# HGRN scores and outputs written between the k tiles of the projections that follow

## The chip, the cores and the metric

The kernel runs on one core of a Trainium2 chip. A core has five engines with a queue each: PE (TensorE, matrix products; the profile shows its weight loads apart, as PEld), DVE (VectorE, elementwise), ACT (ScalarE, functions and scaled copies), POOL (GpSimd) and SP (SyncE, which here issues the DMAs of the weights). PE writes to PSUM, from which DVE and ACT read. An engine runs its queue in order; an instruction that waits holds up those behind it on the same engine. The metric is the device time in microseconds; lower is better.

## The reference, cut to what matters

The input has 256 tokens of width 2048. It is normalised and multiplied by one wide weight matrix, whose columns are split into projections. Of these matter here `hq`, `hf` (query and forget gate of the HGRN branch), `hi`, `hg` (its value and output gate), and `aq`, `ak`, `av` of the attention branch. The HGRN branch has 8 heads of 128:

```python
f = sigmoid(hf); g = lb + (1 - lb) * f; log_g = log(g); kk = 1 - g
q = silu(hq) * HG_DK ** -0.5
# for each chunk of 64 tokens, S carried from chunk to chunk:
b = cumsum(log_g)
o_inter = (q * exp(b)) @ S
scores[t, s] = sum_k q[t, k] * exp(b[t, k] - b[s, k]) * kk[s, k]      # s <= t
o = o_inter + scores @ v
S = exp(b_last) * S + (kk * exp(b_last - b)).T @ v
# then
y_a = rms_norm(o, hg_norm_w) * silu(hg)
```

The attention branch, the gated merge of both branches, an output projection and a squared-ReLU MLP follow; the change does not touch them.

## The kernel before, in words

All large products are computed in three parts: each weight tile is read as f32 (`raw`), ACT casts it to a short form (`wh`, line 89), DVE takes the difference (`wl`, line 90), and PE adds up hi x hi, hi x lo and lo x hi. `weights` (line 109) makes these tiles, 16 k tiles to a projection, and asks SP for their DMAs. `gemm` (line 150) is a projection of 512 columns with tokens as rows (`hi`, `hg`, `av`); each k tile takes six matmuls of 128x512. `gemm_t` (line 158) is one of 256 columns with the transposed result (`hf`, `hq`, `aq`, `ak`); each k tile takes four matmuls (lines 170 to 174). Their accumulators are two buffers of two PSUM banks.

The eight HGRN heads are worked in four pairs `u` = 0 to 3, two pairs to a group of 512 columns. `fq(u)` runs the projections `hf` and `hq` of a pair (those of pairs 0 and 1 run earlier) and makes the gate, `kk`, the scan `b` and the query `q`. `v_chunk(g)` and `hg_chunk(g)` run `hi` and `hg` of a group. `hgrn_scores` (line 346) makes the decayed scores of a pair, without a loop over chunks, in five parts:

- blocks of one token: `kk` x `q` into PSUM (line 353), read by DVE into `sd` (lines 354, 355);
- three levels with blocks of 2, 8 and 32 tokens. For each, DVE and ACT make factors `kl` and `qr` (lines 363 to 386), PE multiplies them (line 393, four f32 products, each two instructions of 128x192), and DVE copies what a mask selects into `sd` (line 400, three copies a head);
- the lower left block of 128 x 128 tokens: factors `kc`, `ql` (lines 405 to 416), PE (line 419), and a copy by ACT into `so` (line 422).

`hgrn_out` (line 427) computes a pair's output: PE multiplies the scores by `v` into `po` (lines 439, 440), ACT squares (line 443), DVE and POOL make the reciprocal root (lines 95, 96), DVE scales and gates into `o` (line 450). It returns `finish`, which transposes `o` on PE into `tpo` (line 458) and splits it into the activations `ya` (lines 460, 461). Score tiles and `po` tiles share two PSUM buffers of one bank each (the tag `sm`); a pair's `po` needs both.

Two things set the order. The first is the order in which the program writes its instructions, at the end of the stage (lines 481 to 498). The second is the planner of the framework: in its own model of time it gives every engine, at each point, the instruction that was written first among those whose inputs and buffers are ready by then. The order so made is fixed in each engine's queue. Blocks under `high_priority` count as if written 2000 instructions earlier; the splitting of weights and the emptying of some accumulators are such blocks. So instructions of the scores that are written early may run before, and PE may fit pieces of a later projection between them.

Of the kernel before, what the change touches and what calls it, by code (L numbers as in the profile page):

```python
# [8 lines left out]
F32 = mybir.dt.float32  # L9
# [41 lines left out]
def tile_hybrid_block(  # L51
# [95 lines left out]
    def lhs_of(lhs, kt, m):  # L147
        return [lhs[kt // 4][:, kt % 4, u, m * P:(m + 1) * P] for u in range(2)]

    def gemm(lhs, w, n0, nkt, what, wide=False):  # L150

        acc = new_acc(what)
        for kt, wh, wl in weights(w, n0, nkt, NC, what, wide=wide):
            for m in range(NM):
                mm3(acc[:, m, :], *lhs_of(lhs, kt, m), wh, wl, kt == 0, kt == nkt - 1)
        return acc

    def gemm_t(rhs, w, n0, nkt, what):

        acc = new_acc(what)  # L160
        for a in weights(w, n0, nkt, T, what):
            mm_t(acc, rhs, nkt, *a)
        return acc

    def mm_t(acc, rhs, nkt, kt, wh, wl):
        r = rhs[kt // 4][:, kt % 4]
        for cb in range(2):
            c = slice(cb * P, (cb + 1) * P)
            if kt:
                nc.tensor.matmul(acc[:, cb, 0:T], wl[:, c], r[:, 0, :], start=False, stop=False)  # L170
            nc.tensor.matmul(acc[:, cb, :], wh[:, c], r.rearrange("p u t -> p (u t)"),  # L171
                             start=kt == 0, stop=kt == nkt - 1)
            if kt == 0:
                nc.tensor.matmul(acc[:, cb, 0:T], wl[:, c], r[:, 0, :], start=False, stop=False)
# [149 lines left out]
            nc.vector.tensor_tensor(q[:, h, :, P:], odd(q[:, :, :, 0:P])[:, h], odd(half(g))[:, h], op=ALU.mult)  # L324
        return q

    def v_chunk(g):
        acc = gemm(xT, w_in_n, C_HI + g * NC, KD, f"hi{g}")
        vs = []
        for m in range(NM):  # L330
            v = hp.tile([P, NC], F32, name=f"v{g}{m}", tag="tok", bufs=7)
            nc.scalar.activation(v, acc[:, m, :], AF.Copy, scale=rstd[:, m:m + 1])
            vs.append(v)
        return vs

    def hg_chunk(g):
        acc = gemm(xT, w_in_n, C_HG + g * NC, KD, f"hg{g}")
        gws = []
        for m in range(NM):
            s = hp.tile([P, NC], F32, name=f"gw{g}{m}", tag="tok", bufs=7)  # L340
            nc.scalar.activation(s, acc[:, m, :], AF.Sigmoid, scale=rstd[:, m:m + 1])
            nc.vector.scalar_tensor_tensor(s, acc[:, m, :], rstd[:, m:m + 1], s, op0=ALU.mult, op1=ALU.mult)
            gws.append(s)
        return gws

    def hgrn_scores(n, kk, b, q):

        sd = hp.tile([P, 2, NM, P], F32, name=f"sd{n}", tag="sd", bufs=2)

        for h in range(2):  # L350
            ps = ps_sm.tile([P, NM, 192], F32, name=f"ps{n}_1{h}", tag="sm")
            for m in range(NM):
                nc.tensor.matmul(ps[:, m, :], kk[:, h, m * P:(m + 1) * P], q[:, h, m, :], start=True, stop=True)
            nc.vector.tensor_tensor(sd[:, h], ps[:, :, 0:P], bc(ident, 1, NM), op=ALU.mult)
            nc.vector.copy_predicated(sd[:, h].rearrange("p m (j u) -> p m j u", u=2)[:, :, :, 1],
                                      bc(mask1.bitcast(I32), 1, NM), ps[:, :, P:])

        for i, B in enumerate(LEVELS):
            npar = 2 * T // (4 * B)
            blocks = lambda a: a.rearrange("p h t -> p (h t)").rearrange("p (n v b) -> p n v b", v=4, b=B)  # L360
            bv = blocks(b)
            end = bv[:, :, :, B - 1]
            el = hp.tile([P, npar, 4, B], F32, name=f"el{n}_{B}", tag="e", bufs=2)
            nc.vector.tensor_tensor(el, bc(end, 3, B), bv, op=ALU.subtract)
            nc.scalar.activation(el, el, AF.Exp)
            kl = hp.tile([P, npar, 4, B], F32, name=f"kl{n}_{B}", tag="kl", bufs=3)
            nc.vector.tensor_tensor(kl, blocks(kk), el, op=ALU.mult)
            er = hp.tile([P, npar, 4, B], F32, name=f"er{n}_{B}", tag="e", bufs=2)
            rr = hp.tile([P, npar, 4], F32, name=f"rr{n}_{B}", tag=f"rr{B}", bufs=2)
            if B < CH // 2:  # L370
                nc.vector.tensor_tensor(er[:, :, 1:4, :], bv[:, :, 1:4, :], bc(end[:, :, 0:3], 3, B), op=ALU.subtract)
                nc.scalar.activation(er[:, :, 1:4, :], er[:, :, 1:4, :], AF.Exp)
                nc.vector.tensor_tensor(rr[:, :, 1:3], end[:, :, 1:3], end[:, :, 0:2], op=ALU.subtract)
                nc.scalar.activation(rr[:, :, 1:3], rr[:, :, 1:3], AF.Exp)
            else:
                two = lambda a, j: a.rearrange("p n (w j) b -> p n w j b", j=2)[:, :, :, j, :]
                nc.vector.tensor_tensor(two(er, 1), two(bv, 1), bc(two(bv, 0)[:, :, :, B - 1], 3, B), op=ALU.subtract)
                nc.scalar.activation(two(er, 1), two(er, 1), AF.Exp)
                nc.scalar.activation(two(er, 0), two(bv, 0), AF.Exp)
                nc.vector.tensor_copy(rr, er[:, :, :, B - 1])  # L380
            qr = hp.tile([P, npar, 6, B], F32, name=f"qr{n}_{B}", tag="qr", bufs=2)
            wide = lambda a, k: a.rearrange("p (a n) k b -> p a n (k b)", n=32 // B)[:, :, :, k]
            qv = q[:, :, :, 0:P].rearrange("p h m t -> p (h m) t").rearrange("p a (n w) -> p a n w", w=4 * B)
            nc.vector.tensor_tensor(wide(qr, slice(0, 3 * B)), qv[:, :, :, B:], wide(er, slice(B, 4 * B)), op=ALU.mult)
            nc.vector.tensor_tensor(qr[:, :, 3:5, :], qr[:, :, 1:3, :], bc(rr[:, :, 1:3], 3, B), op=ALU.mult)
            nc.vector.tensor_tensor(qr[:, :, 5, :], qr[:, :, 4, :], bc(rr[:, :, 1], 2, B), op=ALU.mult)
            klf = kl.rearrange("p n v b -> p (n v b)")
            qrf = qr.rearrange("p n k b -> p (n k b)")
            for h in range(2):
                ps = ps_sm.tile([P, NM, 192], F32, name=f"ps{n}_{B}{h}", tag="sm")  # L390
                for m in range(NM):
                    a = 2 * h + m
                    nc.tensor.matmul(ps[:, m, :], klf[:, a * P:(a + 1) * P], qrf[:, a * 192:(a + 1) * 192],  # L393
                                     start=True, stop=True)
                dst = sd[:, h].rearrange("p m (n w) -> p m n w", w=4 * B)
                src = ps.rearrange("p m (n w) -> p m n w", w=6 * B)
                mask = masks[:, i, :].rearrange("p (n w) -> p n w", w=6 * B).bitcast(I32)
                for d0, k0, k1 in ((1, 0, 3), (2, 3, 5), (3, 5, 6)):
                    k = slice(k0 * B, k1 * B)
                    nc.vector.copy_predicated(dst[:, :, :, d0 * B:], bc(mask[:, :, k], 1, NM), src[:, :, :, k])  # L400

        heads = lambda a: a.rearrange("p (h m) v b -> p h m v b", m=NM)
        r = rr.rearrange("p (h m) v -> p h m v", m=NM)
# [10 lines left out]
        ql = hp.tile([P, 2, 4, 32], F32, name=f"ql{n}", tag="ql", bufs=1)  # L414
        nc.vector.tensor_tensor(ql[:, :, 0, :], q[:, :, 1, 0:32], heads(er)[:, :, 1, 0, :], op=ALU.mult)
        nc.vector.tensor_tensor(ql[:, :, 1:4, :], heads(qr)[:, :, 1, 0:3, :], bc(d128[:, :, 1:4], 3, 32), op=ALU.mult)
        ps = ps_sm.tile([P, 2, P], F32, name=f"ps{n}_128", tag="sm")
        for h in range(2):
            nc.tensor.matmul(ps[:, h, :], kc[:, h].rearrange("p v b -> p (v b)"),
                             ql[:, h].rearrange("p v b -> p (v b)"), start=True, stop=True)  # L420
        so = hp.tile([P, 2, P], F32, name=f"so{n}", tag="so", bufs=2)
        nc.scalar.copy(so, ps)
        return sd, so

    ya = []

# [35 lines left out]

        return finish

    def fq(u):
        if u == 0:
            f, z = f0, z0
        elif u == 1:
            f, z = f1, z1
        else:  # L470
            f, z = h2(f"f{u}"), h2(f"zq{u}")
            add_parts(f, gemm_t(xT, w_in_t, C_HF + u * T, KD, f"hf{u}"))
            add_parts(z, gemm_t(xT, w_in_t, C_HQ + u * T, KD, f"hq{u}"))
        g, kk, b = hf_pair(u, f)
        return kk, b, hq_pair(u, z, g)


    def hgrn_group(g, s0, s1, vs, gws):
        return hgrn_out(g, 0, s0, vs, gws), hgrn_out(g, 2, s1, vs, gws)

    ya += [new_act(f"ya{g}") for g in range(2)]
    a0, a1 = fq(0), fq(1)
    vs0 = v_chunk(0)
    gws0 = hg_chunk(0)
    s0 = hgrn_scores(0, *a0)
    a2 = fq(2)
    s1 = hgrn_scores(1, *a1)
    a3 = fq(3)
    o0 = hgrn_group(0, s0, s1, vs0, gws0)
    vs1 = v_chunk(1)  # L490
    for finish in o0:
        finish()
    s2 = hgrn_scores(2, *a2)
    gws1 = hg_chunk(1)
    s3 = hgrn_scores(3, *a3)
    acc_q0 = gemm_t(xT, w_in_t, C_AQ, KD, "aq00")
    for finish in hgrn_group(1, s2, s3, vs1, gws1):
        finish()
    hpool_cm.__exit__(None, None, None)


# [527 lines left out]
```

## Time and profile before

| | |
|---|---|
| median of 3 runs | 1424.85 us (1422.13 to 1425.19) |
| the profiled execution | 1427.49 us |
| its span, first to last instruction | 1425.8 us |
| mean granted clock of TensorE | 0.997 |
| PE busy | 1404.3 us |
| DVE busy | 1147.7 us |
| ACT busy | 855.0 us |
| first score matmul to last, in the span | 98.37 to 227.9 us |
| `po` matmuls | 155.7 to 236.9 us |
| transposes of the outputs | 184.6 to 242.4 us |

Busy time is the sum of an engine's instructions, overlaps counted once; matmuls overlap, and their ends are modelled. In a row of the timeline stand the start, the length, the engine, the line, the operation and its tiles, and in brackets how long the engine had been idle before and which instruction released it. In a row of the groups `x96` is a count and the last column the idle time before them. In the windows each row is a stretch; the granted clock is 1.00 where PE runs at full speed.

### The profile page before, as it was taken

The page shows a single profiled execution, that of the slowest core. Times are in us where ns is not written, and L with a number is a line of the kernel's source. Part 1 is how long each engine was busy: PE and PEld are TensorE (multiplying, and loading weights), DVE is VectorE, ACT ScalarE, POOL GpSimd, SP SyncE. Part 2 cuts the span into 40 slices and gives each one's busy share as a digit, 9 for nine tenths or more (in the row PEclk, how much of TensorE's full clock was granted, in tenths as well). Part 3 has the DMA queues.
Part 4 walks back from the last instruction along what each step waited for, and adds up shares of the span by engine and source line. Part 5 has one row for each costly group of instructions (what it writes and reads, how often), then busy time and mean ns, then how long its engine had stood idle before and what let it go on. Part 6 is the DMA issues. An engine that isn't in the chain of part 4 may idle for free.

```text
span 1425.8 us, 18422 instructions
## 1 busy us (share of the span) xinstructions
PE 1404.3 (98%) x6629; PEld 1162.4 (82%) x6629; DVE 1147.7 (80%) x1506; ACT 855.0 (60%) x1132; POOL 33.9 (2%) x92
## 2 busy tenths in 40 slices
PE   9999999999999999999999999999999999999997
PEld 7888788878787888888888878888788888888886
DVE  7779886675758885688998978979788998889984
ACT  6766744464556664446666765566556775557753
POOL 2000001010000000000000000000000000000000
PEclk9999999999999999999999999999999999999999
DMA  9654444565556657656654566555576555667542
GB/s 315 231 192 148 134 161 133 189 177 167 163 177 222 212 185 226 202 194 222 207 191 133 192 223 215 182 187 177 184 236 236 178 167 173 234 223 237 180 146 103
DMA packets 122156, 272.83 MB, mean 191 GB/s; under 512 B 10192, under 2 KB 31440, under 8 KB 121680
## 3 DMA queue, kind: packets, MB, share of 16 engines
q1 hardware_dynamic: 119328, 264.80, 56.0%
q0 software_dynamic: 1584, 5.25, 1.4%
q10 hardware_dynamic: 1152, 1.60, 0.3%
q8 instruction: 52, 0.85, 0.2%
q14 instruction: 40, 0.33, 0.1%
HBM read 269.51 MB, written 2.10 MB: 190 GB/s over the span
## 4 chain that ended last, share of the span: by engine, by line
PE 77%; DVE 10%; DMA 5%; ACT 3%; issue 3%; SPq 1%; POOL 0%; POOLq 0%; ACTq 0%; DVEq 0%
PE acc_ak L171 2%; PE acc_aq L171 2%; DVE raw_dn L702 2%; PE acc_hf L171 1%; PE acc_hq L171 1%; PE ps L393 1%; PE acc_hg L145 1%; PE acc_hg L144 1%; PE acc_hg L143 1%; PE acc_ba L145 1%; PE acc_bb L143 1%; PE acc_av L145 1%; PE acc_bb L144 1%; PE acc_ba L144 1%; PE acc_av L143 1%
## 5 line engine op out<-in xcount | busy, mean ns | idle before, releaser
L171 PE MATMUL acc_hf<-act_x,wh_hf 128*128 128x512 f32 x128 | 47.2, 405 | 1.3 <-DVE f L179 1.3
L171 PE MATMUL acc_aq<-act_x,wh_aq 128*128 128x512 f32 x128 | 47.1, 404 | 0.0
L171 PE MATMUL acc_hq<-act_x,wh_hq 128*128 128x512 f32 x128 | 45.9, 398 | 0.0
L171 PE MATMUL acc_ak<-act_x,wh_ak 128*128 128x512 f32 x128 | 45.0, 397 | 0.0
L702 DVE TENSOR_TENSOR raw_up<-raw_up,raw_up 128x1024 f32<-128x1024 f32 x32 | 39.1, 1221 | 0.5
L702 DVE TENSOR_TENSOR raw_dn<-raw_dn,raw_dn 128x1024 f32<-128x1024 f32 x32 | 39.0, 1218 | 0.2
L90 DVE TENSOR_TENSOR wl_ga<-raw_ga,wh_ga 128x1024 fp32r<-128x1024 f32 x16 | 19.6, 1225 | 19.6 <-ACT wh_ga L89 19.6
L170 PE MATMUL acc_aq<-act_x,wl_aq 128*128 128x256 f32 x120 | 35.1, 293 | 0.0
L170 PE MATMUL acc_hf<-act_x,wl_hf 128*128 128x256 f32 x120 | 34.8, 290 | 0.0
L90 DVE TENSOR_TENSOR wl_av<-raw_av,wh_av 128x1024 fp32r<-128x1024 f32 x16 | 19.6, 1224 | 18.1 <-ACT wh_av L89 18.1
L170 PE MATMUL acc_ak<-act_x,wl_ak 128*128 128x256 f32 x120 | 33.6, 280 | 0.0
L170 PE MATMUL acc_hq<-act_x,wl_hq 128*128 128x256 f32 x120 | 33.6, 280 | 0.0
L90 DVE TENSOR_TENSOR wl_ba<-raw_ba,wh_ba 128x1024 fp32r<-128x1024 f32 x16 | 19.6, 1224 | 16.6 <-ACT wh_ba L89 16.6
L89 ACT CAST wh_ba<-raw_ba 128x1024 fp32r<-128x1024 f32 x16 | 16.9, 1053 | 24.3 <-PE acc_ba L145 10.0
L90 DVE TENSOR_TENSOR wl_bb<-raw_bb,wh_bb 128x1024 fp32r<-128x1024 f32 x16 | 19.6, 1222 | 14.7 <-ACT wh_bb L89 14.7
L89 ACT CAST wh_bb<-raw_bb 128x1024 fp32r<-128x1024 f32 x16 | 16.9, 1054 | 22.8 <-PE acc_ba L145 12.7
L89 ACT CAST wh_av<-raw_av 128x1024 fp32r<-128x1024 f32 x16 | 16.8, 1052 | 22.0 <-PE acc_av L145 12.4
L90 DVE TENSOR_TENSOR wl_aq<-raw_aq,wh_aq 128x1024 fp32r<-128x1024 f32 x16 | 19.6, 1224 | 12.6 <-ACT wh_aq L89 12.6
L171 PEld LDWEIGHTS acc_hf<-act_x,wh_hf 128*128 128x128 f32 x128 | 24.2, 189 | 6.5 <-DVE f L179 1.6
L171 PEld LDWEIGHTS acc_hq<-act_x,wh_hq 128*128 128x128 f32 x128 | 24.0, 188 | 5.5
L171 PEld LDWEIGHTS acc_ak<-act_x,wh_ak 128*128 128x128 f32 x128 | 23.9, 188 | 5.5
L171 PEld LDWEIGHTS acc_aq<-act_x,wh_aq 128*128 128x128 f32 x128 | 24.1, 188 | 5.2 <-issue 0.7
(1626 smaller groups left out, 5107.3 us busy)
## 6 DMA issues: line engine op xcount, KB each, us to landing
raw_up<-in_w_up_dram SPq DMA_DIRECT2D x32, 512.0 KB, 5.4
raw_dn<-in_w_down_dram SPq DMA_DIRECT2D x32, 512.0 KB, 5.6
raw_ga<-in_w_in_t_dram SPq DMA_DIRECT2D x20, 512.0 KB, 4.4
raw_hi<-in_w_in_n_dram SPq DMA_DIRECT2D x16, 512.0 KB, 4.5
raw_hg<-in_w_in_n_dram SPq DMA_DIRECT2D x16, 512.0 KB, 3.7
raw_aq<-in_w_in_t_dram SPq DMA_DIRECT2D x16, 512.0 KB, 4.3
raw_ak<-in_w_in_t_dram SPq DMA_DIRECT2D x16, 512.0 KB, 3.6
raw_av<-in_w_in_n_dram SPq DMA_DIRECT2D x16, 512.0 KB, 4.3
```

The source lines that it names most:

```text
L89: (copy or nc.scalar.copy)(hi, src)
L90: nc.vector.tensor_tensor(lo, src, hi.bitcast(F32), op=ALU.subtract)
L143: nc.tensor.matmul(acc, hi, wh, start=first, stop=False, skip_group_check=True)
L144: nc.tensor.matmul(acc, hi, wl, start=False, stop=False, skip_group_check=True)
L145: nc.tensor.matmul(acc, lo, wh, start=False, stop=last, skip_group_check=True)
L170: nc.tensor.matmul(acc[:, cb, 0:T], wl[:, c], r[:, 0, :], start=False, stop=False)
L171: nc.tensor.matmul(acc[:, cb, :], wh[:, c], r.rearrange("p u t -> p (u t)"), start=kt == 0, stop=kt == nkt - 1)
L393: nc.tensor.matmul(ps[:, m, :], klf[:, a * P:(a + 1) * P], qrf[:, a * 192:(a + 1) * 192], start=True, stop=True)
L702: nc.vector.tensor_tensor(dst, dst, t, op=ALU.add)
```

## The change

No instruction of the computation is added or removed. `hgrn_scores` becomes a generator that stops at six places, and `gemm` and `gemm_t` take a list `between` of pairs (k tile, function): before the matmuls of that k tile are written, the function is called once. The first stop is after the factors of the level of 2; then come the blocks of one token and the factors of 8; the matmuls of level 2 and the factors of 32; those of level 8 and the factors `kc`, `ql`; those of level 32; and the block of 128. Factors are thus written one step ahead of the matmuls that use them, where before each level's factors stood right ahead of its matmuls.

Where each is written, with its k tiles:

| | before | after |
|---|---|---|
| scores of pair 0 | behind `hg0` | inside `hg0`, at 0, 5, 7, 9, 11, 13 |
| scores of pair 1 | behind `hq2` and the work of pair 2 | inside `hf2` at 0, 2, 6, 11 and `hq2` at 1, 6 |
| output of pair 0 | behind `hq3` and the work of pair 3 | inside `hq2` at 12 |
| output of pair 1 | right behind that of pair 0 | inside `hf3` at 8 |
| transposes of pairs 0 and 1 | behind `hi1` | inside `hq3` at 6 and 12 |
| scores of pair 2 | behind `hi1` and those transposes | inside `hi1` at 0, 5, 7, 9, 11, 13 |
| scores of pair 3 | behind `hg1` | inside `hg1` at 0, 5, 7, 9, 11, 13 |
| output of pair 2 | behind `aq00` | inside `aq00` at 6 |
| output of pair 3, both transposes | behind `aq00` | behind `aq00` |

```diff
-    def gemm(lhs, w, n0, nkt, what, wide=False):
+    def gemm(lhs, w, n0, nkt, what, wide=False, between=None):
 
         acc = new_acc(what)
         for kt, wh, wl in weights(w, n0, nkt, NC, what, wide=wide):
+            if between and between[0][0] == kt:
+                between.pop(0)[1]()
             for m in range(NM):
                 mm3(acc[:, m, :], *lhs_of(lhs, kt, m), wh, wl, kt == 0, kt == nkt - 1)
         return acc
 
-    def gemm_t(rhs, w, n0, nkt, what):
+    def gemm_t(rhs, w, n0, nkt, what, between=None):
 
         acc = new_acc(what)
         for a in weights(w, n0, nkt, T, what):
+            if between and between[0][0] == a[0]:
+                between.pop(0)[1]()
             mm_t(acc, rhs, nkt, *a)
         return acc
...
-    def hgrn_scores(n, kk, b, q):
+    def hgrn_scores(n, kk, b, q, out):
 
         sd = hp.tile([P, 2, NM, P], F32, name=f"sd{n}", tag="sd", bufs=2)
 
-        for h in range(2):
...
-        for i, B in enumerate(LEVELS):
+        def factors(B):
+
             npar = 2 * T // (4 * B)
...
+            return kl, qr, er, rr
+
+        def level(i, B, kl, qr):
             klf = kl.rearrange("p n v b -> p (n v b)")
...
+        made = factors(LEVELS[0])
+        yield
+
+        for h in range(2):
+            ps = ps_sm.tile([P, NM, 192], F32, name=f"ps{n}_1{h}", tag="sm")
+            for m in range(NM):
+                nc.tensor.matmul(ps[:, m, :], kk[:, h, m * P:(m + 1) * P], q[:, h, m, :], start=True, stop=True)
...
+        for i, B in enumerate(LEVELS):
+            kl, qr, er, rr = made
+            if i < len(LEVELS) - 1:
+                made = factors(LEVELS[i + 1])
+                yield
+                level(i, B, kl, qr)
...
+        yield
+        level(len(LEVELS) - 1, B, kl, qr)
+        yield
         ps = ps_sm.tile([P, 2, P], F32, name=f"ps{n}_128", tag="sm")
...
-        return sd, so
+        out += [sd, so]
+        yield
...
-    def hgrn_group(g, s0, s1, vs, gws):
-        return hgrn_out(g, 0, s0, vs, gws), hgrn_out(g, 2, s1, vs, gws)
-
     ya += [new_act(f"ya{g}") for g in range(2)]
-    a0, a1 = fq(0), fq(1)
-    vs0 = v_chunk(0)
-    gws0 = hg_chunk(0)
-    s0 = hgrn_scores(0, *a0)
-    a2 = fq(2)
-    s1 = hgrn_scores(1, *a1)
-    a3 = fq(3)
-    o0 = hgrn_group(0, s0, s1, vs0, gws0)
-    vs1 = v_chunk(1)
-    for finish in o0:
-        finish()
-    s2 = hgrn_scores(2, *a2)
-    gws1 = hg_chunk(1)
-    s3 = hgrn_scores(3, *a3)
-    acc_q0 = gemm_t(xT, w_in_t, C_AQ, KD, "aq00")
-    for finish in hgrn_group(1, s2, s3, vs1, gws1):
-        finish()
+    a, sc, vs, gws, ends = [None] * 4, [[] for _ in range(4)], [None] * 2, [None] * 2, []
+
+    def scores(u, *at):
+
+        steps = hgrn_scores(u, *a[u], sc[u])
+        return [(k, lambda: next(steps)) for k in at]
+
+    def outputs(u):
+        ends.append(hgrn_out(u // 2, u % 2 * 2, sc[u], vs[u // 2], gws[u // 2]))
+
+    def end():
+        ends.pop(0)()
+
+    a[0], a[1] = fq(0), fq(1)
+    vs[0] = v_chunk(0)
+    gws[0] = hg_chunk(0, scores(0, 0, 5, 7, 9, 11, 13))
+    s1 = scores(1, 0, 2, 6, 11, 1, 6)
+    a[2] = fq(2, s1[:4], s1[4:] + [(12, lambda: outputs(0))])
+    a[3] = fq(3, [(8, lambda: outputs(1))], [(6, end), (12, end)])
+    vs[1] = v_chunk(1, scores(2, 0, 5, 7, 9, 11, 13))
+    gws[1] = hg_chunk(1, scores(3, 0, 5, 7, 9, 11, 13))
+    acc_q0 = gemm_t(xT, w_in_t, C_AQ, KD, "aq00", [(6, lambda: outputs(2))])
+    outputs(3)
+    end()
+    end()
```

More of the change, by code (lines that the diff above doesn't have):

```diff
@@ L325, in hq_pair, with v_chunk @@
         return q
-    def v_chunk(g):
-        acc = gemm(xT, w_in_n, C_HI + g * NC, KD, f"hi{g}")
+    def v_chunk(g, between=None):
+        acc = gemm(xT, w_in_n, C_HI + g * NC, KD, f"hi{g}", between=between)
         vs = []
@@ L334, in v_chunk, with hg_chunk @@
         return vs
-    def hg_chunk(g):
-        acc = gemm(xT, w_in_n, C_HG + g * NC, KD, f"hg{g}")
+    def hg_chunk(g, between=None):
+        acc = gemm(xT, w_in_n, C_HG + g * NC, KD, f"hg{g}", between=between)
         gws = []
@@ L344, in hg_chunk @@
         return gws
-    def hgrn_scores(n, kk, b, q):
+    def hgrn_scores(n, kk, b, q, out):
         sd = hp.tile([P, 2, NM, P], F32, name=f"sd{n}", tag="sd", bufs=2)
-        for h in range(2):
[L351 to L356, printed above, removed]
-        for i, B in enumerate(LEVELS):
+        def factors(B):
             npar = 2 * T // (4 * B)
@@ L400, in hgrn_scores @@
                     nc.vector.copy_predicated(dst[:, :, :, d0 * B:], bc(mask[:, :, k], 1, NM), src[:, :, :, k])
+        made = factors(LEVELS[0])
[4 more added lines that the diff above has]
+                nc.tensor.matmul(ps[:, m, :], kk[:, h, m * P:(m + 1) * P], q[:, h, m, :], start=True, stop=True)
+            nc.vector.tensor_tensor(sd[:, h], ps[:, :, 0:P], bc(ident, 1, NM), op=ALU.mult)
+            nc.vector.copy_predicated(sd[:, h].rearrange("p m (j u) -> p m j u", u=2)[:, :, :, 1],
+                                      bc(mask1.bitcast(I32), 1, NM), ps[:, :, P:])
+        for i, B in enumerate(LEVELS):
[4 more added lines that the diff above has]
+                level(i, B, kl, qr)
         heads = lambda a: a.rearrange("p (h m) v b -> p h m v b", m=NM)
@@ L463, in hgrn_out, with fq @@
         return finish
-    def fq(u):
+    def fq(u, first=None, second=None):
         if u == 0:
@@ L471, in fq @@
             f, z = h2(f"f{u}"), h2(f"zq{u}")
-            add_parts(f, gemm_t(xT, w_in_t, C_HF + u * T, KD, f"hf{u}"))
-            add_parts(z, gemm_t(xT, w_in_t, C_HQ + u * T, KD, f"hq{u}"))
+            add_parts(f, gemm_t(xT, w_in_t, C_HF + u * T, KD, f"hf{u}", first))
+            add_parts(z, gemm_t(xT, w_in_t, C_HQ + u * T, KD, f"hq{u}", second))
         g, kk, b = hf_pair(u, f)
         return kk, b, hq_pair(u, z, g)
-    def hgrn_group(g, s0, s1, vs, gws):
-        return hgrn_out(g, 0, s0, vs, gws), hgrn_out(g, 2, s1, vs, gws)
     ya += [new_act(f"ya{g}") for g in range(2)]
-    a0, a1 = fq(0), fq(1)
-    vs0 = v_chunk(0)
-    gws0 = hg_chunk(0)
-    s0 = hgrn_scores(0, *a0)
-    a2 = fq(2)
-    s1 = hgrn_scores(1, *a1)
-    a3 = fq(3)
-    o0 = hgrn_group(0, s0, s1, vs0, gws0)
-    vs1 = v_chunk(1)
-    for finish in o0:
-        finish()
-    s2 = hgrn_scores(2, *a2)
-    gws1 = hg_chunk(1)
-    s3 = hgrn_scores(3, *a3)
-    acc_q0 = gemm_t(xT, w_in_t, C_AQ, KD, "aq00")
-    for finish in hgrn_group(1, s2, s3, vs1, gws1):
-        finish()
+    a, sc, vs, gws, ends = [None] * 4, [[] for _ in range(4)], [None] * 2, [None] * 2, []
[18 more added lines that the diff above has]
+    end()
     hpool_cm.__exit__(None, None, None)
```

## The prediction

> **What bounds the kernel now.** I read the page from the top: the span, the busy rows, the clock row, the chain by engine.
>
> ```profile
> span 1425.8 us, 18422 instructions
> PE 1404.3 (98%) x6629; PEld 1162.4 (82%) x6629; DVE 1147.7 (80%) x1506; ACT 855.0 (60%) x1132; POOL 33.9 (2%) x92
> PEclk9999999999999999999999999999999999999999
> PE 77%; DVE 10%; DMA 5%; ACT 3%; issue 3%; SPq 1%; POOL 0%; POOLq 0%; ACTq 0%; DVEq 0%
> ```
>
> PE is busy 98% of the span and carries 77% of the chain. 1425.8 - 1404.3 = 21.5 us are all the time in which it has nothing, so a change that removes no matmul can win only a part of that, and what a slowed clock or a change of matmul kind costs. The change touches 54 to 248 us. What PE waited for from 98 us on, in the view of waits:
>
> ```profile
> PE po L440 <- DVE o L450: 2.6, 1, 2.6
> PE tpo L458 <- DVE o L450: 2.0, 2, 1.0
> PE ps L393 <- DVE sd L355: 0.6, 1, 0.6
> ```
>
> So 5.2 us, 4.6 of them in the outputs, not in the scores. The windows view gives busy time by stretch (stretch and length; then PE, PEld, DVE, ACT, POOL busy; the granted clock; DMA):
>
> ```profile
> 83.00:98.00 15.00, 15.00 (x68) 12.43 (x67) 9.02 (x14) 6.78 (x7) 0.00 (x0) 1.00 0.72 237
> 126.70:156.99 30.29, 29.72 (x177) 26.49 (x176) 28.67 (x69) 21.12 (x27) 0.00 (x0) 1.00 0.44 144
> 156.00:185.00 29.00, 26.36 (x125) 22.10 (x123) 21.69 (x47) 18.37 (x37) 2.71 (x2) 0.94 0.45 145
> 161.60:164.23 2.63, 0.00 (x0) 0.00 (x0) 1.71 (x7) 1.72 (x3) 1.59 (x1) 0.92 0.02 8
> 164.23:167.55 3.32, 3.32 (x14) 3.18 (x15) 3.07 (x7) 0.63 (x4) 0.00 (x0) 0.55 0.02 5
> 184.60:213.57 28.97, 28.97 (x141) 24.07 (x140) 25.50 (x61) 14.33 (x21) 0.00 (x0) 1.00 0.45 146
> 230.87:248.05 17.18, 15.18 (x97) 13.24 (x96) 10.67 (x22) 8.64 (x25) 4.06 (x8) 1.00 0.50 146
> ```
>
> The hole is 161.60 to 164.23, and behind it PE works 3.32 us at a clock of 0.55: 3.32 x 0.45 = 1.5 us more. The other thing to see is DVE, second only to PE here: 28.67 of 30.29 us while the second pair's scores run, 25.50 of 28.97 with the third's, but 9.02 of 15 just before the first pair's scores begin.
>
> The rows of the waits, from the timeline (start, length, instruction; in brackets the idle time before it and who ended it), PE first, then POOL and DVE:
>
> ```profile
> 132.66 0.89 PE L393 MATMUL ps<-qr,kl 128*128 128x192 f32 x4 [0.57 <-DVE sd L355]
> ...
> 155.74 0.60 PE L440 MATMUL po<-v,sd 128*128 128x128 f32 x4
> ...
> 156.99 0.47 PE L143 MATMUL acc_hi<-wh_hi,act_x 128*128 128x512 f32 x1
> ...
> 164.23 1.22 PE L440 MATMUL po<-v,sd 128*128 128x128 f32 x4 [2.64 <-DVE o L450]
> ...
> 230.87 0.60 PE L440 MATMUL po<-v,sd 128*128 128x128 f32 x4
> ...
> 235.08 0.33 PE L458 MATMUL tpo<-ident,o 128*128 128x128 f32 x1 [0.96 <-DVE o L450]
> ...
> 239.70 0.30 PE L458 MATMUL tpo<-ident,o 128*128 128x128 f32 x1 [1.04 <-DVE o L450]
> ```
>
> ```profile
> 161.94 1.59 POOL L96 TENSOR_TENSOR ro<-ms,mhalf 128x4 f32<-128x4 f32 x1 [122.63 <-DVE ms L95]
> ```
>
> ```profile
> 163.57 1.13 DVE L450 SCALAR_TENSOR_TENSOR o<-po,ro,gw 128x128 f32<-128x128 f32 x4 [0.92 <-POOL ro L96]
> ...
> 234.67 1.13 DVE L450 SCALAR_TENSOR_TENSOR o<-po,ro,gw 128x128 f32<-128x128 f32 x4 [1.12 <-POOL ro L96]
> ```
>
> A pair's output is a chain: `po` matmuls, squares on ACT, the power on POOL, `o` on DVE. From the first `po` to the end of `o` it took 163.57 + 1.13 - 155.74 = 9.0 us the first time, 234.67 + 1.13 - 230.87 = 4.9 us the third. The two `po` tiles fill both small PSUM buffers, so the next pair's `po` stands on PE until that chain is through, and everything behind it stands too.
>
> **The change, part by part.** No instruction is added or removed, no DMA is issued by a moved step, and SP's stream of weights keeps its order. Moved are PE, DVE and ACT instructions of the scores, the four powers on POOL, and the transposes. I take each place in turn, and first how far apart the new places are:
>
> ```profile
> 98.37 1.46 PE L353 MATMUL ps<-q,kk 128*128 128x192 f32 x8
> 99.53 0.53 PE L171 MATMUL acc_hf<-act_x,wh_hf 128*128 128x512 f32 x1
> 99.90 0.28 PE L174 MATMUL acc_hf<-act_x,wl_hf 128*128 128x256 f32 x1
> 100.01 0.40 PE L171 MATMUL acc_hf<-act_x,wh_hf 128*128 128x512 f32 x1
> 100.25 0.28 PE L174 MATMUL acc_hf<-act_x,wl_hf 128*128 128x256 f32 x1
> ...
> 115.59 0.40 PE L171 MATMUL acc_hq<-act_x,wh_hq 128*128 128x512 f32 x1
> ...
> 126.70 1.46 PE L353 MATMUL ps<-q,kk 128*128 128x192 f32 x8
> ...
> 227.22 0.68 PE L419 MATMUL ps<-ql,kc 128*128 128x128 f32 x4
> ```
>
> ```profile
> L143 PE MATMUL acc_hg<-wh_hg,act_x x64: 387/389/532, 76.6 to 212.9; 128*128 128x512 f32 x64
> ```
>
> A k tile of a transposed projection (`hf`, `hq`, `aq`) lasts (126.70 - 115.59) / 16 = 0.69 us, one of `hi` or `hg` (98.37 - 76.6) / 16 = 1.36 us.
>
> The hole at 161.60. Pair 0's `po` now stands at k tile 12 of `hq2`, pair 1's at k tile 8 of `hf3`: 12 tiles, 12 x 0.69 = 8.3 us, and pair 0's own `po` matmuls, 156.99 - 155.74 = 1.25 us, make 9.5 us between the two. The chain took 9.0 us at its longest and 4.9 at its shortest, so the wait of 2.6 us becomes 0 to 2.6; I take 0.3, since even the slow chain fits. Gain 2.3 us. Late next is `hq2`'s own end, whose accumulator is emptied as before.
>
> The slowed clock. It came once, in the 3.3 us behind the longest hole; the waits of 0.57, 0.96 and 1.04 us lie in stretches of clock 1.00. With the hole gone I take the 1.5 us as gained; ends 0 and 1.5. The Trainium skill, "TensorE: Matmul & The Clock Gate", section "Why this matters for your kernels", asks for no idle gaps over about 3 us between bursts of matmuls. Here 2.63 us were enough, so the trace does not agree with that limit. Taken by the rule, the slow stretch would not belong to this hole and could stay; the sum would then be 1.5 us smaller.
>
> The end of the stage. Pair 2's `po` moves from behind `aq00` to its k tile 6: 10 tiles x 0.69 = 6.9 us ahead of pair 3's, against a chain of 4.9 us in this place. Its transposes are then ready when they are written, and its wait of 0.96 us goes. Pair 3's is written as before, behind `aq00`; its transposes still wait for its `o`, as the row at 239.70 does: 1.0 us stays. Gain 1.0, ends 0 and 2.0. The transposes of pairs 0 and 1 move from behind `hi1` into `hq3`; there `o` is long done (8 x 0.69 + 6 x 0.69 us behind pair 1's `po`), and they cost what they cost before.
>
> The scores' steps. Before, the first level follows as soon as it is ready, so it often goes in two halves, one per head, with a piece of a projection between. Each return from a small f32 group to a projection costs PE 0.13 us: 99.53 to 99.90 is 0.37 us where 100.01 to 100.25 is 0.24. Counting groups in the timeline, from the one at 98.37 to the one at 227.22, I find 30 in the four pairs; written in five steps of both heads there can be 20. 10 x 0.13 = 1.3 us at best, none if both heads still find one buffer taken; I take 0.6. The wait of 0.57 us at 132.66 goes with it: 0.3 taken, 0 to 0.6.
>
> New waits. Twenty steps stand at fixed places. Each one's matmuls need factors that are written one step earlier or more, and DVE must read both PSUM tiles of the step before. The least distance is 2 x 0.69 us plus nothing (in `hf2`, k tile 0 to 2, where only factors are due), else 2.7 us or more and the step's own 1.16 us. The trace has one wait of 0.57 us in its 30 groups; with that rate the twenty would cost 0.4 us; I take 0.6, and as the other end 20 x 0.57 = 11.4.
>
> Two covers are counted at nothing. Pair 0's level work goes from 99-112 us back into `hg0`, where DVE works 9.02 of 15 us: 6.0 us free. The DVE work of levels from this row,
>
> ```profile
> L400 DVE COPY_PREDICATED sd<-masks,ps 128x128 f32<-128x128 int32 (+2 forms) x72 | 18.5, 311 | 1.4 <-PE ps L393 1.0
> ```
>
> is 18.5 / 4 = 4.6 us a pair and fits. The third pair's goes into `hi1`, where DVE had 21.69 of 29.00 us: 21.7 + 4.6 = 26.3, on a stretch that loses its hole and gains 5 us of score matmuls; it fits, with little to spare. If it did not, weights would come late and PE would wait.
>
> **Sum.** 2.3 + 1.5 + 1.0 + 0.6 + 0.3 - 0.6 = 5.1 us. The profiled execution took 1427.49 us, 1.7 more than its span, and is 2.6 above the median of 1424.85. Against itself it becomes 1422.4, span 1420.7; against the median 1419.7. All terms at their good end (2.6 + 1.5 + 2.0 + 1.3 + 0.6) give 8.0 us, 1416.8.
>
> **The rivals.** About 0.2%, 2.85 us, is what a measurement of this kernel can tell from no change.
>
> A: the waits come back at the new places. The order on PE is fixed ahead by planned durations, and the hole at 161.60 shows that the plan thought `o` ready 2.6 us before it was. If ACT and DVE are as crowded in `hq2` and `hf3` (28.67 of 30.29 us says so), pair 1's `po` waits again, and the slow stretch follows. Left are 1.0 + 0.6 + 0.3 - 0.6 = 1.3 us: 1423.5. Against it: 9.5 us of distance, where there was none.
>
> B, on the other side: DVE becomes the bound inside the projections. A score matmul that waits stops the projection behind it. With the observed 0.57 us at each of 20 steps the 0.6 us of new waits become 11.4: 1419.7 + 10.8 = 1430.5. It decides from 0.28 us a step, where 5.7 us eat the gains. For it: DVE at 95% in 126.70:156.99. Against it: the third pair, before, already runs its levels inside `hg1` at the same density, five steps in 16 us, without a wait:
>
> ```profile
> 185.00 1.47 PE L353 MATMUL ps<-q,kk 128*128 128x192 f32 x8
> ...
> 199.74 0.60 PE L419 MATMUL ps<-ql,kc 128*128 128x128 f32 x4
> ```
>
> C: the many small groups slow the clock. Were one stretch like 164.23:167.55 to come with each pair's scores, four would cost 4 x 1.5 = 6.0 us, and the time would be 1425.7, no change. The Trainium skill, same page, section "A second HAM failure mode: psum-queue depth-cycling", tells of a kernel whose short idles between groups that cycle through PSUM banks made the clock drop again and again; that speaks against this change. By that rule, 1425.7. The trace bears it out little: 126.70:156.99 and 184.60:213.57 hold such groups and a granted clock of 1.00.
>
> D: everything goes, pair 3's wait with it: 1416.8.
>
> **How the numbers follow.** The forecast, near 1419.7 (1417.3 to 1421.9), 0.54; D and better 0.08; A, and mixtures of it with small new waits (1422 to 1424.5), 0.17; C and the like (to 1427.7) 0.06; B 0.15. Faster by over 0.2% (below 1422.0) is the forecast, D and a little of A: 0.63. Same: most of A, and C: 0.21. Slower: B and a rest, 0.16. The range goes from 1416.6 to 1425.8; outside are B and a little of D. The forecast's own range is 1417.3 to 1421.9.
>
> **What would show it.** Right, if PE's waits on DVE `o` between 98 and 250 us fall from 4.6 to about 1.3 us, if no stretch has a clock of 0.5, if `L393` waits under 1 us in all, if the groups of score matmuls are x8 rather than x4, and if `ak` begins about 5 us before 248. Wrong, if `po` still waits over 2 us, if PE waits at `ps` for `sd` or `qr` sum to over 5 us, if DVE's weight differences (`wl`) hold PE, or if the stage is 5 us shorter and the time is not.

## The result, and the profile after

The changed kernel took 1418.03 us (median of 4 runs, 1416.87 to 1419.64), the kernel before, with one more run beside those shown, 1425.02 us. The medians differ by 7.0 us; the ratio on record is 0.9957, 95% interval 0.9945 to 0.9969. Two later series of the same two kernels gave 0.9966 (0.9954 to 0.9979) and 0.9971 (0.9961 to 0.9982), with medians 5.5 and 4.2 us apart. So the gain is some 4 to 7 us; 5.1 had been forecast. The profiled execution took 1417.60 us. The same lines of its page:

```profile
span 1415.9 us, 18431 instructions
PE 1399.4 (99%) x6629; PEld 1160.7 (82%) x6629; DVE 1148.7 (81%) x1506; ACT 856.1 (60%) x1133; POOL 34.0 (2%) x92
PE 88%; DVE 6%; DMA 2%; issue 2%; ACT 2%; POOL 0%; SPq 0%; POOLq 0%; DVEq 0%; ACTq 0%
```

PE has the same 6629 matmuls, and it carries 88% of the chain instead of 77%. What PE waited for between 98 and 250 us, in the view of waits of the changed kernel:

```profile
PE tpo L479 <- DVE act_ya L482: 1.4, 2, 0.8
PE ps L393 <- DVE sd L410: 1.3, 1, 1.3
```

Every wait on `o` is gone; two others are new. The span shrank by 9.9 us, more than the time: two tile views, of the first matmuls of `hi` and of `ak` (count, shortest, median and longest in ns, first and last start), show how much of that is the stage. First the kernel before:

```profile
L143 PE MATMUL acc_hi<-wh_hi,act_x x64: 387/389/473, 54.8 to 183.9; 128*128 128x512 f32 x64
...
L171 PE MATMUL acc_ak<-act_x,wh_ak x128: 387/396/403, 248.1 to 349.1; 128*128 128x512 f32 x128
```

Then the changed one:

```profile
L143 PE MATMUL acc_hi<-wh_hi,act_x x64: 387/389/530, 53.0 to 185.6; 128*128 128x512 f32 x64
...
L175 PE MATMUL acc_ak<-act_x,wh_ak x128: 387/396/403, 240.7 to 341.8; 128*128 128x512 f32 x128
```

From the start of `hi0` to the start of `ak` are 193.3 us before and 187.7 after: 5.6 us less. The other 4.3 us lie ahead of the stage (54.8 against 53.0) and behind it, and are not the change's: two more profiles of the changed kernel have `hi0` at 53.5 and 53.8, the run with no tail wait, whose source is the same up to `hi0`, has it at 54.8, and from `ak` to the last `dn32` row 1168.0 and 1167.3 us where the first has 1165.3 and the kernel before 1167.8. The stage itself took 187.6 us in both, so its length repeats within 0.1 us and tells more than the time of one run. It is the measure below.

The windows that answer to those of before (stretch and length; PE, PEld, DVE, ACT, POOL; clock; DMA), `hf3` with `hq3`, `hi1`, and `aq00` with `aq01`:

```profile
130.00:157.00 27.00, 26.19 (x159) 22.96 (x158) 24.80 (x48) 22.63 (x38) 2.27 (x2) 1.00 0.47 157
157.00:184.00 27.00, 25.66 (x125) 21.79 (x124) 25.54 (x64) 15.61 (x21) 0.00 (x0) 1.00 0.43 139
213.70:240.70 27.00, 26.43 (x163) 23.22 (x162) 18.68 (x31) 15.30 (x32) 4.07 (x8) 1.00 0.51 172
```

The clock is 1.00 throughout; the stretch of 0.55 is gone. DVE is at 25.54 of 27.00 us in `hi1`, and there PE now waits. The rows of PE in the timeline, then of DVE:

```profile
127.47 0.60 PE L461 MATMUL po<-v,sd 128*128 128x128 f32 x4
...
137.15 0.61 PE L461 MATMUL po<-v,sd 128*128 128x128 f32 x4
...
154.51 0.41 PE L479 MATMUL tpo<-ident,o 128*128 128x128 f32 x2 [0.81 <-DVE act_ya L482]
...
169.49 1.54 PE L393 MATMUL ps<-qr,kl 128*128 128x192 f32 x8 [1.34 <-DVE sd L410]
...
226.30 0.60 PE L461 MATMUL po<-v,sd 128*128 128x128 f32 x4
...
231.63 0.44 PE L479 MATMUL tpo<-ident,o 128*128 128x128 f32 x2 [0.57 <-DVE act_ya L482]
```

```profile
131.28 1.13 DVE L471 SCALAR_TENSOR_TENSOR o<-po,ro,gw 128x128 f32<-128x128 f32 x4 [1.14 <-POOL ro L96]
...
148.10 0.35 DVE L471 SCALAR_TENSOR_TENSOR o<-po,ro,gw 128x128 f32<-128x128 f32 x1
```

No `po` waits any more. Pair 0's chain took 131.28 + 1.13 - 127.47 = 4.9 us, half of the 9.0 before. Pair 1's took 148.10 + 0.35 - 137.15 = 11.3 us, longer than any before, and no `po` stood behind it.

### The profile page after: what moved, and what is told of

It is laid out like the page before. It is cut to its first block, busy times and chain, and to the rows that moved or that the text cites. A ratio compares the mean times of both kernels' runs of the same rounds, so it can differ in the third digit from the quotient of the medians.

```text
span 1415.9 us, 18431 instructions
## 1 busy us (share of the span) xinstructions
PE 1399.4 (99%) x6629; PEld 1160.7 (82%) x6629; DVE 1148.7 (81%) x1506; ACT 856.1 (60%) x1133; POOL 34.0 (2%) x92
## 4 chain that ended last, share of the span: by engine, by line
PE 88%; DVE 6%; DMA 2%; issue 2%; ACT 2%; POOL 0%; SPq 0%; POOLq 0%; DVEq 0%; ACTq 0%
PE acc_ak L175 2%; PE acc_aq L175 2%; PE acc_hf L175 2%; PE acc_hq L175 2%; PE ps L393 1%; PE acc_hg L145 1%; PE acc_hg L143 1%; PE acc_hg L144 1%; PE acc_ba L145 1%; PE acc_av L144 1%; PE acc_bb L143 1%; PE acc_bb L145 1%; PE acc_ba L144 1%; PE acc_bb L144 1%; PE acc_av L143 1%
## 5 line engine op out<-in xcount | busy, mean ns | idle before, releaser
L89 ACT CAST wh_aq<-raw_aq 128x1024 fp32r<-128x1024 f32 x16 | 16.8, 1050 | 19.5 <-PE acc_hg L145 8.6
```

Of the source, the lines that this page charges most:

```text
L89: (copy or nc.scalar.copy)(hi, src)
```

## The experiments

All runs, with the ratio to the kernel before on the same chip and the length of the stage:

| run | ratio, 95% interval | `hi0` to `ak`, us |
|---|---|---|
| before | 1 | 193.3 |
| changed, first / again / third | 0.9957 / 0.9966 / 0.9971 | 187.7 / 187.6 / 187.6 |
| outputs alone | 0.9981 (0.9972 to 0.9990) | 190.6 |
| scores alone | 0.9966 (0.9953 to 0.9978) | 189.1 |
| no distance between the outputs | 0.9960 (0.9947 to 0.9972) | 187.5 |
| tail undone | 0.9971 (0.9961 to 0.9981) | 189.4 |
| heads apart | 0.9971 (0.9959 to 0.9983) | 188.2 |
| all steps in one place | 0.9988 (0.9979 to 0.9997) | 191.5 |
| later steps | 0.9958 (0.9945 to 0.9970) | 186.0 |
| distance alone | 0.9973 (0.9964 to 0.9982) | 188.9 |
| no tail wait | 0.9963 (0.9951 to 0.9976) | 186.1 |

My theory was that the outputs make the gain, by the distance between them. The rival was that the scores make it: their steps, and their earlier place, which takes load off ACT and DVE.

### The two halves alone

```diff
 # outputs alone, from the kernel before
-    a2 = fq(2)
+    a2 = fq(2, None, [(12, lambda: outputs(0, s0, vs0, gws0))])
     s1 = hgrn_scores(1, *a1)
-    a3 = fq(3)
+    a3 = fq(3, [(8, lambda: outputs(1, s1, vs0, gws0))], [(6, end), (12, end)])
...
-    acc_q0 = gemm_t(xT, w_in_t, C_AQ, KD, "aq00")
+    acc_q0 = gemm_t(xT, w_in_t, C_AQ, KD, "aq00", [(6, lambda: outputs(2, s2, vs1, gws1))])
```

> Outputs and their transposes moved into the projections as in the changed kernel, the scores left whole and where they were. If the gain is the outputs' (my theory): PE's wait of 2.6 us on o before po goes, no stretch of clock 0.5 follows, the tail waits fall from 2.0 to about 1; 4 to 5.5 us faster than before. If the gain is the scores' steps and their earlier place: not more than 1.5 us faster.

```diff
 # scores alone, from the changed kernel
-    a[2] = fq(2, s1[:4], s1[4:] + [(12, lambda: outputs(0))])
-    a[3] = fq(3, [(8, lambda: outputs(1))], [(6, end), (12, end)])
+    a[2] = fq(2, s1[:4], s1[4:])
+    a[3] = fq(3)
+    outputs(0)
+    outputs(1)
...
-    acc_q0 = gemm_t(xT, w_in_t, C_AQ, KD, "aq00", [(6, lambda: outputs(2))])
+    acc_q0 = gemm_t(xT, w_in_t, C_AQ, KD, "aq00")
+    outputs(2)
```

> Scores in steps inside the projections, the outputs written where they were before. My theory: the wait of po on o stays at 2 to 3 us with a slow stretch behind it, the tail waits stay near 2; only the returns from small groups are saved (20 groups for 30), 1 to 2 us faster than before. If the earlier scores themselves freed ACT and DVE so that o comes in time: the wait is under 1 us, no slow stretch, 4 us faster or more.

Neither side was right, though the scores alone came near to what the rival had expected of them. The outputs alone shorten the stage by 2.7 us, the scores alone by 4.2; together 5.6, less than the sum of 6.9. PE's row of the scores alone, with the outputs where they were:

```profile
159.26 0.71 PE L461 MATMUL po<-v,sd 128*128 128x128 f32 x4 [1.28 <-DVE o L471]
```

The hole is half as long as before (2.64), and no slow stretch follows. Pair 0's chain has shortened from 9.0 to 7.1 us. What had made it long stands in ACT's rows of the kernel before:

```profile
157.78 0.21 ACT L443 ACTIVATION_READ_ACCUMULATOR osq<-po 128x1 f32 x1
158.01 1.28 ACT L308 ACT_TABLE_LOAD   x1
159.31 0.63 ACT L308 ACTIVATE lg<-f 128x512 f32<-128x512 f32 x1
159.84 0.26 ACT L443 ACTIVATE osq<-po 128x128 f32<-128x128 f32 x1
```

Between the pair's first two squares and its last two, ACT loads a function table (1.28 us) and makes the logarithm `lg` of the gate of pair 3, just projected. In the scores alone the four squares follow one another, and the table load comes behind them. Only the scores were moved in that run, so their move has changed this order in the plan; by what step is not shown.

Both halves do away with the slowed clock, and both with a part of the hole, so their gains can't add up. The outputs alone lose elsewhere a part of what they win there: in the view of waits `tpo` waits 2.6 us on `o` at three places, `ps` 0.8 us on `o`. How the 1.3 us of overlap divide is not shown.

### The hole and the clock

```diff
 # distance alone, from the kernel before
-    o0 = hgrn_group(0, s0, s1, vs0, gws0)
-    vs1 = v_chunk(1)
+    o0 = [hgrn_out(0, 0, s0, vs0, gws0)]
+    vs1 = v_chunk(1, [(8, lambda: o0.append(hgrn_out(0, 2, s1, vs0, gws0)))])
```

> The kernel before with one edit: the output of pair 1 written at k tile 8 of hi1 instead of right behind that of pair 0; scores, tail and transposes as before. It takes the hole alone away. If the hole and the slow clock behind it are one cost: from the start of hi0 to the start of ak 193.3 - 2.8 - 1.6 = 188.9 us, no stretch of clock 0.5 before the end, and about 4 us faster than before. If the slow stretch has another cause: the hole goes, the stretch stays, 2.5 to 3 us faster.

```profile
L143 PE MATMUL acc_hi<-wh_hi,act_x x64: 389/389/479, 53.0 to 177.7; 128*128 128x512 f32 x64
...
L173 PE MATMUL acc_ak<-act_x,wh_ak x128: 387/396/403, 241.9 to 343.0; 128*128 128x512 f32 x128
```

188.9 us, as expected: 4.4 us for one edit, and no stretch below 1.00 in the stage. In the timeline of the kernel before, the last rows ahead of the hole are

```profile
160.97 0.39 PE L145 MATMUL acc_hi<-wh_hi,act_x 128*128 128x512 f32 x1
161.20 0.39 PE L143 MATMUL acc_hi<-wh_hi,act_x 128*128 128x512 f32 x1
```

From 161.20 to the `po` at 164.23 are 3.0 us where 0.23 is usual, so the hole was worth 2.8 us, the clock the other 1.6. Hole and slow stretch went together.

Whether a hole of this length slows the clock seems to be partly chance, though. The first two of these windows (columns as in the windows above) are from the hole of the kernel before. The other two lie behind the last matmul of the whole kernel: the third row is from the changed kernel's third profile, where that matmul ends at 1409.5, the fourth from the scores alone, where it ends at 1409.7.

```profile
161.60:163.80 2.20, 0.00 (x0) 0.00 (x0) 1.28 (x5) 1.72 (x3) 1.59 (x1) 1.00 0.02 9
163.80:164.20 0.40, 0.00 (x0) 0.00 (x0) 0.40 (x3) 0.00 (x0) 0.00 (x0) 0.51 0.00 0
...
1409.60:1414.10 4.50, 0.00 (x0) 0.00 (x0) 2.11 (x5) 2.06 (x4) 0.56 (x1) 1.00 0.74 270
...
1412.20:1412.70 0.50, 0.00 (x0) 0.00 (x0) 0.47 (x2) 0.48 (x1) 0.00 (x0) 0.52 0.71 254
```

In the hole the clock fell after 2.2 us without a matmul; at the ends of the thirteen traces it fell after 2.5 us (scores alone) to 4.8 us (changed, third). So another execution of the kernel before may pass the same hole at full clock. Its 50 runs beside the experiments suggest this: 33 have a mean granted clock of 0.997 or less and took 1426.1 us on average, 17 have 0.998 or more and took 1424.1; all 66 runs of the nine edited kernels have 0.998 or more. The sign is not clean, as 4 of the changed kernel's 16 runs have 0.997 too. The profiled execution had the slow stretch. If it comes in two executions of three, the change saves 4.0 + 2/3 x 1.6 = 5.1 us on average (an estimate), not 5.6.

```diff
 # no distance, from the changed kernel
-    a[2] = fq(2, s1[:4], s1[4:] + [(12, lambda: outputs(0))])
-    a[3] = fq(3, [(8, lambda: outputs(1))], [(6, end), (12, end)])
+    a[2] = fq(2, s1[:4], s1[4:] + [(12, lambda: (outputs(0), outputs(1)))])
+    a[3] = fq(3, None, [(6, end), (12, end)])
```

> The changed kernel with the output of pair 1 written right behind that of pair 0 (both at k tile 12 of hq2) instead of 12 k tiles later. If the distance matters: PE waits 2 to 3 us before the second po, and a slow stretch of 3.4 us follows; 3 to 4.5 us slower than the changed kernel, about 3 us faster than before. If the place alone matters: no wait over 0.5 us, as fast as the changed kernel.

```profile
132.45 0.71 PE L461 MATMUL po<-v,sd 128*128 128x128 f32 x4 [0.90 <-DVE o L471]
```

187.5 us, not longer than the changed kernel. The wait on `o` is there, but 0.9 us, and the new waits are smaller in return (0.61 us of `ps` on `sd`, 0.6 of `tpo`). At the new place the distance gains nothing: the chain takes 4.9 us there, and the planner fills most of it. The second `po` starts 4.5 us behind the first (at 127.97), 0.9 of them the wait.

### The tail

```diff
 # tail undone, from the changed kernel
-    acc_q0 = gemm_t(xT, w_in_t, C_AQ, KD, "aq00", [(6, lambda: outputs(2))])
+    acc_q0 = gemm_t(xT, w_in_t, C_AQ, KD, "aq00")
+    outputs(2)
     outputs(3)
```

> The changed kernel with the output of pair 2 back behind aq00, next to that of pair 3. My theory: two waits of about 1 us on o return in front of the transposes, 1 to 1.8 us slower than the changed kernel. If other work covers them: within 0.5 us of it.

```profile
PE tpo L479 <- DVE o L471: 2.1, 2, 1.1
```

The two waits return, and the stage is 1.8 us longer: as expected. In the view of waits 2.1 us stand in place of 0.6, so 0.3 of the 1.8 don't show there.

### The steps of the scores

```diff
 # heads apart, from the changed kernel: a stop after the first head of each step
-                level(i, B, kl, qr)
+                level(i, B, kl, qr, [0])
+                yield
+                level(i, B, kl, qr, [1])
...
-    gws[0] = hg_chunk(0, scores(0, 0, 5, 7, 9, 11, 13))
-    s1 = scores(1, 0, 2, 6, 11, 1, 6)
+    gws[0] = hg_chunk(0, scores(0, 0, 5, 6, 7, 8, 9, 10, 11, 12, 13))
+    s1 = scores(1, 0, 2, 4, 6, 8, 11, 13, 1, 3, 6)
...
```

> The changed kernel with the two heads of each score step written one k tile apart (ten steps a pair instead of five, the last at the same k tile): 16 more returns from a small f32 group to a projection. If a return costs PE 0.13 us: 2.1 us slower than the changed kernel, and 0.37 instead of 0.24 us to the second matmul behind each group. If the returns cost nothing: within 0.5 us of it, unless waits of PE on the scores' tiles differ.

The timeline has 36 groups where the changed kernel has 20, and each return shows its 0.13 us; yet the stage is only 0.6 us longer, 0.035 us a group. The rows of heads apart and of the changed kernel say why:

```profile
85.45 0.81 PE L393 MATMUL ps<-qr,kl 128*128 128x192 f32 x4
85.97 0.53 PE L143 MATMUL acc_hg<-wh_hg,act_x 128*128 128x512 f32 x1
86.34 0.39 PE L144 MATMUL acc_hg<-wl_hg,act_x 128*128 128x512 f32 x1
```

```profile
85.64 1.47 PE L393 MATMUL ps<-qr,kl 128*128 128x192 f32 x8
86.81 0.53 PE L143 MATMUL acc_hg<-wh_hg,act_x 128*128 128x512 f32 x1
```

A group of eight takes 1.17 us from its start to the next row's, a group of four 0.52. Two groups of four take 1.04, which gives back 0.13 us: what is paid on the way out is saved on the way in.

```diff
 # all steps in one place, from the changed kernel
-        return [(k, lambda: next(steps)) for k in at]
+        return [(at[0], lambda: next(steps)), (at[1], lambda: [next(steps) for _ in range(5)])]
...
```

> The changed kernel with all steps of a pair but the first factors written in one place, at k tile 5 (pair 1: 2) of the projection. If the spacing of the steps is worth something: heads split again into groups of four, waits of PE on the scores' tiles of 0.3 to 0.6 us each, 1.5 to 3 us slower than the changed kernel. If only the earlier place matters: within 0.5 us of it.

```profile
86.33 0.89 PE L393 MATMUL ps<-qr,kl 128*128 128x192 f32 x4 [1.77 <-DVE sd L410]
```

191.5 us, 3.9 more than the changed kernel; 27 groups, and 3.3 us of waits of `ps` on `sd` instead of 1.3. So the spacing is worth 3.9 us: moved earlier without it, the scores leave PE waiting on DVE. The waits explain 2.0 us, seven more groups 0.2; in the view of waits the weight loads of the scores (`L393`, `L439`) stand idle 6.7 us instead of 1.7, part of it the same waits seen twice. How the remaining 1.7 us divide stays open.

```diff
 # later steps, from the changed kernel
-    a[3] = fq(3, [(8, lambda: outputs(1))], [(6, end), (12, end)])
-    vs[1] = v_chunk(1, scores(2, 0, 5, 7, 9, 11, 13))
+    a[3] = fq(3, [(8, lambda: outputs(1))], [(2, end), (12, end)])
+    vs[1] = v_chunk(1, scores(2, 0, 5, 8, 10, 12, 14))
```

> The changed kernel with pair 2's steps at k tiles 0, 5, 8, 10, 12, 14 of hi1 and the first transposes at 2 instead of 6 of hq3. If the two new waits (1.34 us of ps on sd, 0.81 us of tpo on ya) come from steps that stand too close for DVE: both go, 1.5 to 2.2 us faster than the changed kernel. If the plan only moves DVE's lateness on: the waits come back elsewhere and the time stays within 0.7 us.

```profile
PE tpo L479 <- DVE act_ya L482: 0.6, 1, 0.6
PE ps L393 <- DVE sd L400: 0.4, 1, 0.4
```

With four of pair 2's steps one k tile later and the transposes four earlier, 1.34 us of wait become 0.41, and the 0.81 go: 186.0 us, 1.6 less than the changed kernel. Which of the two moves took which wait away was not run apart. In time it took 1419.25 us (1417.37 to 1420.45) where the changed kernel, on the same chip, took 1419.98 (1419.80 to 1420.72): the difference has the right sign, but five runs don't tell it from none.

> The changed kernel once more, on the chip of these runs: 6 to 7 us faster than before. It is the measure for the three others.

```diff
 # no tail wait, from later steps
-    acc_q0 = gemm_t(xT, w_in_t, C_AQ, KD, "aq00", [(6, lambda: outputs(2))])
+    acc_q0 = gemm_t(xT, w_in_t, C_AQ, KD, "aq00", [(6, lambda: outputs(2)), (13, end)])
     outputs(3)
-    end()
     end()
```

> The run with later steps, and pair 2's transposes at k tile 13 of aq00 as well. If the last wait (0.57 us of tpo on ya) is the two pairs' transposes standing next to each other on two PSUM buffers: it goes, and from the start of hi0 to the start of ak it takes 185.2 us where the run with later steps took 186.0 and the changed kernel 187.6; 1.5 to 2.5 us faster than the changed kernel. If pair 3's own chain bounds them: 186.0.

```profile
231.09 0.30 PE L479 MATMUL tpo<-ident,o 128*128 128x128 f32 x1 [1.08 <-DVE o L471]
```

186.1 us: the wait on `ya` went, and one of 1.08 us on pair 3's `o` took its place. Pair 3's own chain bounds the end of the stage, as its rival had it. The time was 1419.04 us (1418.05 to 1420.51) against 1420.28 (1418.70 to 1421.90) of the changed kernel beside it; again the ranges overlap.

> The changed kernel as the measure on this chip: 187.6 us from hi0 to ak, 5 to 7 us faster than before.

## Why the prediction was right

The forecast was 5.1 us; the stage lost 5.6, and the three series lie at 4.1 to 6.1 by their ratios (1425 x 0.0029 and x 0.0043). The places of the gain were right, several sizes were not, and their errors nearly cancelled: +0.6 us for the hole and the clock, +0.8 for the tail, +0.05 for the scores' groups and their old wait, -1.0 for the new waits. That the sum came so near is in part luck. Step by step:

**The hole and the slowed clock.** Forecast 2.3 + 1.5 = 3.8 us, measured 4.4 by the edit that removes nothing else. The mechanism was right, the hole mis-sized by 0.5: I took the idle time in the brackets, which begins at the modelled end of the last matmul, and left 0.3 us of it standing. The distance from start to start counts; for the hole it is 2.8 us. But the reason I gave for it, twelve k tiles of distance against a chain of 9.0 us, was not what was needed: without the distance the changed kernel is as fast. At the end of `hq2` the chain takes 4.9 us. Distance alone, with the chain still at 9.0 us, took the hole away; the emptier place without distance left 0.9 us of it and no slow stretch. The change has both. And the scores, for whose steps and old wait my sum had 0.6 + 0.3 us, shorten the stage by 4.2 us alone, mostly because moving them shortens this chain too: that was not in my sum.

**The rule on idle gaps.** The limit of about 3 us in the Trainium skill, "TensorE: Matmul & The Clock Gate", section "Why this matters for your kernels", was weighed against the row of 2.63 us. The runs side with the row: the slow stretch went with the hole of 2.64 us, and behind holes of 1.28 and 1.77 us, in the scores alone and in one place, there is none. By the rule 1.5 us less had been due. But no fixed limit shows: the clock fell after 2.2 us of idle time in the hole, and after up to 4.8 us at the ends of the traces. I had taken the whole 1.5 us, where the runs of the kernel before suggest two executions of three.

**The tail.** Forecast 1.0, measured 1.8 by undoing it. The mechanism was right, the size not: I let pair 3's wait of 1.0 us stay whole, and 0.57 us stayed, on `ya` instead of `o`.

**The returns from small groups.** Forecast 0.6 of a possible 1.3. The groups fell from 30 to 20 as said, but a group costs 0.035 us and not 0.13, so ten give 0.35, if that price holds for them. The term's price was the failed part: I had read the extra 0.13 us behind a group and not the saving in its first rows.

**The new waits.** Forecast 0.6, seen 1.34 + 0.81 = 2.2 us; later steps took 1.6 us of that off again. The step that failed is the cover counted at nothing in `hi1`, "it fits, with little to spare": DVE is at 25.54 of 27.00 us there, and PE waited 1.34 us for it. The 0.81 us lie at the transposes in `hq3`, of which the prediction said that they cost what they cost before. The other cover, `hg0`, held: no wait in it.

The sum of what was measured, 4.4 + 1.8 + 0.35 + 0.6 for the old wait of `ps` - 1.6 = 5.5, answers to the 5.6. That supports the account and does not prove it: the edits start from different kernels, the 0.35 and the 0.6 are readings and not edits of their own, and the clock's part holds for the profiled execution. Of the signs named in advance one missed: `L393` was to wait under 1 us in all, and waited 1.34.

**The rivals.** A did not come: no `po` waits, and without the distance only 0.9 us. C did not: the clock is 1.00 through the stage in the changed kernel, and with 36 groups too. What the section "A second HAM failure mode: psum-queue depth-cycling" of the same page of the Trainium skill tells of another kernel, which would have made it 1425.7, was not seen in any profile here. B is what happens without the spacing: the run with all steps in one place is the slowest of the changed ones, though still faster than before. D did not come: three waits are left.

## What to carry to other kernels

Where a producer's output waits for a chain over other engines, look at what those engines do at that place: moving the chain to where they had less to do shortened it from 9.0 to 4.9 us, and there the distance between the two outputs gained nothing more. Work fitted between the k tiles of a product wants a spacing in which the second busiest engine, here DVE, can keep up: without it the stage took 3.9 us more. To judge gains of a few us, measure the length of the stage between two landmarks of the trace, which here repeated within 0.1 us while whole runs spread over 3 us. But one profile does not show what varies from execution to execution, as the slowed clock did here.

## What had not been expected

A hole of 2.64 us cost 4.4 us in the profiled execution, because 3.3 us at a clock of 0.55 followed it; behind holes of 1.77 us and less the clock stayed at 1.00. How long PE had to be idle before the clock fell was not the same each time: 2.2 us in this hole, 2.5 to 4.8 us at the ends of the traces. And the price of switching between a projection and small f32 groups, 0.13 us in the rows behind each group, was nearly undone in the group itself: 16 more groups cost 0.6 us, not 2.1.
